# Value projection of a hybrid decoder block: four of six jobs as seven block products, a layer norm by token halves, and multiplications of the merge on GpSimd

## The chip, the cores and the metric

The kernel runs on one core of a Trainium2 chip. Its engines work at the same time, each through its own list of instructions in order: TensorE (PE in the profile, with its weight loads as PEld), VectorE (DVE), ScalarE (ACT), GpSimd (POOL) and SyncE (SP), which issues nearly all transfers between the on-chip memory (SBUF) and device memory. TensorE writes its products into eight banks of a second memory (PSUM), which VectorE and ScalarE read. The metric is the device time of one execution in microseconds. Of three runs of the kernel before the median is 1675.62 us (1674.95 to 1675.65). What VectorE can compute and what the scheduling helpers do is told below as far as the change touches it.

## The reference

One decoder layer on 1024 tokens of width 1024. What matters here is its first half:

```python
h = rms_norm(x, g_pre_mix[l])
z = h @ w_in[l]
q, k, v, glu_in, z_ga, z_gc = jnp.split(z, ...)     # v: 1024 x 1536
y_attn = dilated_attention_mixer(q, k, v, ...)       # 3 groups x 8 heads of 64, windows of 128 keys
y_conv = conformer_conv_mixer(glu_in, ...)           # GLU, causal depthwise conv, layer_norm, silu, @ w_conv_out
merged = sigmoid(z_ga) * y_attn + sigmoid(z_gc) * y_conv
x = x + rms_norm(merged @ w_mix_out[l], g_post_mix[l])
x = x + rms_norm(swiglu_ffn(rms_norm(x, g_pre_ffn[l]), ...), g_post_ffn[l])
```

The three attention groups have their own outputs per head; they are merged per head and token with weights that come from the softmax denominators. The layer norm of the convolution branch takes mean and variance over the 1024 channels of each token.

## The kernel before, in words

**Precision.** All matrix products are float32 products made of three: each operand is split in a high part (a copy rounded to the type fp32r, made by ScalarE) and a low part (operand minus high part, made by VectorE or GpSimd). A product is high by high, high by low and low by high. So each operand costs one copy and one subtraction before TensorE may use it.

**Seven products for eight.** The projections for the convolution input, the gates, the queries and the keys, and the first feed-forward matrix, use Winograd's form of Strassen's scheme (`winograd`, `prod`): a matrix product is cut in 2 x 2 blocks, and seven block products of sums of blocks replace eight. The sums of the token operand (named T1 to T4, with B11, B21, B22) are made once, in `block_sums`, and kept in `B.T`; the sums of the weights (S1 to S4, with A11, A12, A22) are made for each pair of weight tiles in `quarters`, with the splits in `both`.

**Order.** The program writes the instructions of all engines in the order of TensorE's work. TensorE's loops call `tick()` after every few products. A list of steps due at a tick (`later`), and generators that go one step further at ticks (`bg`), put the other engines' work and the transfers between them. The attention is a generator of its own, `fine`: `beat()` is called several times for each product of the value, gate and convolution-output stages, adds RATE to a credit, and for each whole credit the attention goes one step further. RATE is RV in the value stage and RU after it. Each engine then runs its list in order, whatever the others do, and waits by semaphore where its data are not there.

**The part of the program around the change**, in TensorE's order:

- Query and key projections (`qk_pair`), with the last of the depthwise convolution on VectorE beside them.
- The value stage: six jobs (`v`), each the values of one group and four of its heads, 1024 tokens by 1024 features by 256 columns. For each of eight blocks of 128 tokens it does eight steps of the features (L1139, L1140): the token block's high part is the stationary operand against 512 moving columns (the weights' high and low part side by side, made by `value_weights`), and its low part against the 256 high columns. ScalarE copies the bank (L1150), GpSimd adds the two halves (L1161), and SyncE stores the values in the layout that the group's attention reads.
- `conv_norm`, a generator in the value stage: the layer norm of the convolution's eight channel blocks, each loaded whole (128 channels by 1024 tokens). Mean, squares, their sums, `rstd` (a few small products, a square root with a Newton step, transposes that spread the result), the multiplication, and silu; the results go to device memory (`d_act`).
- The attention (`attention` with `att_s`, `att_e`, `att_t`, `att_p`, `att_o`), which starts when the layer norm is done: 96 pipelined steps. A step has the scores (L1262, L1266), their minimum on VectorE (L1270), the exponential on ScalarE (L1280), transposes of the scores of four steps before (L1305), the split of the transposed ones (ScalarE L1312, VectorE L1313), the products with the values (L1339), and the addition of the two parts of the result (ScalarE L1354, VectorE L1370). GpSimd prepares the keys (`double`, L1078 to L1080) and the values (`value_parts`, L1110, L1111). Its steps are strewn among the products of the value stage, of one more gate (`plain_gate`) and of the first part of the convolution output.
- The convolution output (`unit`, L336 to L338, 16 units of 24 products), with the silu results loaded and split by `conv_split` and the weights split by `part` (L196, L197).
- `merge`, four generators, one for each pair of heads: the three groups' outputs are loaded again, each multiplied by its weights (L1442, L1446, L1456) and added (L1451, L1461), and the sum is split (`both`, L214, L215) into `OT`. They may multiply only once the attention has ended, in turn.
- The attention output (`unit` again, 16 units of 12 products), which needs all four `OT` from its first unit on: the fourth step of the features reads `OT[3]`. Then the mixing product (L2026), norms, and the feed-forward part.

The lines that hold the value stage's products and its feed:

```python
nc.tensor.matmul(ps, a, w, start=kt == 0, stop=kt == KT - 1, skip_group_check=True)           # L1139
nc.tensor.matmul(ps[:, 256:], b, w[:, :256], start=False, stop=kt == KT - 1, ...)             # L1140
```

## Time and profile before

| what | value |
|---|---|
| median of three runs | 1675.62 us |
| profiled execution, its own time | 1676.75 us |
| its span, first to last instruction | 1675.0 us |
| granted TensorE clock | 0.999 |
| busy share of the span | PE 99%, PEld 83%, DVE 76%, ACT 49%, POOL 32% |
| value stage begins, first L1139 | 544.2 us |
| first attention step, first L1262 | 608.5 us |
| convolution output begins | 792.2 us |
| attention output begins, first product with `OT` | 901.0 us |

The page counts a product as busy from its start to a modelled end. In the value stage one that starts every 0.12 to 0.24 us has a length of 0.28 to 0.40 us, so products overlap in the record, and 99% busy does not mean that none could start earlier. What TensorE does in a stretch is better told by the distance from start to start. A window of the profile with busy time, number of instructions, and idle time before each group shows the other engines.

### The profile page before, as it was taken

To read this page: it belongs to the slowest core of one execution; us is meant where nothing else is said; L and a number is where in the kernel's file an instruction comes from. 1 tells how busy PE (TensorE), PEld (TensorE's weight loads), DVE (VectorE), ACT (ScalarE), POOL (GpSimd) and SP (SyncE) were. 2 spreads that over 40 slices of the span, in tenths; PEclk is the share of its full clock that TensorE was granted. 3 is DMA by queue.
4 is the path that set the end of the run, shared out by engine and by line. 5 is a ranking of instruction groups with operands and counts; after the bars stand their busy time and mean duration, and the time that the engine had idled before them with its cause. 6 is when DMAs were issued, how large, how long until landed. Compare 5 with 4: busy or idle time off the path is not lost.

```text
span 1675.0 us, 23388 instructions
## 1 busy us (share of the span) xinstructions
PE 1658.9 (99%) x8027; PEld 1384.6 (83%) x8027; DVE 1272.3 (76%) x2268; ACT 828.3 (49%) x1646; POOL 542.5 (32%) x456
## 2 busy tenths in 40 slices
PE   9999999999999999999999999999999999999998
PEld 7787888888888889988788888888888888888886
DVE  7998987789899768778876746877655566576686
ACT  7454443443444588888713357633333333354453
POOL 0038777787876366877300300000000000000000
PEclk9999999999999999999999999999999999999999
DMA  4435433455566987879998524134232223494334
GB/s 182 153 102 187 143 132 126 153 176 192 177 176 161 286 273 224 257 220 286 297 272 310 176 88 171 56 132 151 84 118 94 95 95 119 165 375 120 115 119 157
DMA packets 165178, 289.64 MB, mean 173 GB/s; under 512 B 47689, under 2 KB 79812, under 8 KB 165060
## 3 DMA queue, kind: packets, MB, share of 16 engines
q1 hardware_dynamic: 164420, 287.45, 52.5%
q8 instruction: 63, 1.03, 0.3%
q14 instruction: 55, 0.45, 0.1%
q10 hardware_dynamic: 288, 0.52, 0.1%
q0 software_dynamic: 352, 0.18, 0.1%
HBM read 197.39 MB, written 95.42 MB: 175 GB/s over the span
## 4 chain that ended last, share of the span: by engine, by line
PE 87%; issue 5%; DVE 2%; POOL 2%; ACT 2%; DMA 1%; SPq 0%; DVEq 0%; ACTq 0%; POOLq 0%
PE p L354 16%; PE p L353 16%; PE p L352 16%; PE p L2282 13%; PE p L2026 5%; PE p L1139 5%; PE p L336 2%; PE p L337 2%; PE p L338 2%; PE p L1140 2%; PE p L655 2%; PE p L1339 2%; PE p L1305 1%; PE p L1266 1%; PE p L1262 1%
## 5 line engine op out<-in xcount | busy, mean ns | idle before, releaser
L352 PE MATMUL p<-b,b 128*128 128x512 f32 x1316 | 512.7, 390 | 0.1
L354 PE MATMUL p<-b,b 128*128 128x512 f32 x1316 | 512.4, 389 | 0.2
L353 PE MATMUL p<-b,b 128*128 128x512 f32 x1316 | 512.2, 389 | 0.1
L352 PEld LDWEIGHTS p<-b,b 128*128 128x128 f32 x1316 | 247.1, 188 | 52.7 <-ACT c L411 0.5
L354 PEld LDWEIGHTS p<-b,b 128*128 128x128 f32 x1316 | 247.1, 188 | 52.5 <-POOL b L215 1.5
L353 PEld LDWEIGHTS p<-b,b 128*128 128x128 f32 x1316 | 247.1, 188 | 51.7 <-DVE b L1477 0.5
L2282 PE MATMUL p<-b,b 128*128 128x512 f32 x924 | 209.6, 389 | 0.0
L2282 PEld LDWEIGHTS p<-b,b 128*128 128x128 f32 x924 | 173.5, 188 | 36.0
L868 DVE SCALAR_TENSOR_TENSOR p<-b,par,p 128x511 f32<-128x511 f32 (+14 forms) x232 | 163.6, 738 | 0.0
L1139 PE MATMUL p<-b,b 128*128 128x512 f32 x384 | 144.2, 408 | 0.1
L214 ACT CAST b<-d 128x1024 fp32r<-128x1024 f32 x82 | 86.1, 1050 | 100.7 <-POOL d L237 56.6
L215 POOL TENSOR_TENSOR b<-d,b 128x1024 fp32r<-128x1024 f32 x43 | 104.2, 2422 | 47.6 <-ACT b L214 39.0
L1477 DVE TENSOR_TENSOR b<-b,b 128x512 fp32r<-128x512 f32 x141 | 98.9, 708 | 16.0 <-ACT b L1476 14.4
L215 DVE TENSOR_TENSOR b<-d,b 128x1024 fp32r<-128x1024 f32 x39 | 47.6, 1221 | 79.3 <-ACT b L214 79.3
L1140 PE MATMUL p<-b,b 128*128 128x256 f32 x384 | 107.7, 280 | 0.0
L1476 ACT CAST b<-b 128x512 fp32r<-128x512 f32 x141 | 86.4, 619 | 40.9 <-PE p L2282 18.5
L336 PE MATMUL p<-b,b 128*128 128x512 f32 x240 | 96.3, 401 | 0.0
L214 ACT CAST b<-b 128x1024 fp32r<-128x1024 f32 x51 | 53.6, 1052 | 85.0 <-POOL b L246 38.7
L1280 ACT ACTIVATE c<-c,stat 128x128 f32<-128x128 f32 (+1 forms) x192 | 85.2, 447 | 18.2 <-DVE stat L1270 16.9
L337 PE MATMUL p<-b,b 128*128 128x512 f32 x240 | 93.6, 390 | 0.0
L338 PE MATMUL p<-b,b 128*128 128x512 f32 x240 | 93.6, 390 | 0.0
L2026 PE MATMUL p<-b,b 128*128 128x512 f32 x384 | 89.9, 392 | 0.0
(248 smaller groups left out, 2897.0 us busy)
## 6 DMA issues: line engine op xcount, KB each, us to landing
b<-w_in SPq DMA_DIRECT2D x33, 512.0 KB, 5.8
b<-w_fi SPq DMA_DIRECT2D x29, 512.0 KB, 4.4
d<-w_in SPq DMA_DIRECT2D x25, 512.0 KB, 4.2
dk<-c SPq DMA_DIRECT2D x48, 256.0 KB, 4.3
dq<-c SPq DMA_DIRECT2D x48, 256.0 KB, 3.6
b<-dk SPq DMA_DIRECT2D x48, 256.0 KB, 6.2
d<-w_fi SPq DMA_DIRECT2D x22, 512.0 KB, 3.5
dqS<-c SPq DMA_DIRECT2D x44, 256.0 KB, 2.1
```

The costliest lines, as they stand in the source:

```text
L214: self.nc.scalar.copy(hi, x)
L215: self.wsplit.tensor_tensor(lo, x, f(hi), op=OP.subtract)
L336: nc.tensor.matmul(ps, hi[:, s], a, start=kt == 0, stop=False)
L337: nc.tensor.matmul(ps, hi[:, s], b, start=False, stop=False)
L352: nc.tensor.matmul(ps, hi[:, s], a, start=first and kt == 0, stop=False, skip_group_check=True)
L353: nc.tensor.matmul(ps, hi[:, s], b, start=False, stop=False, skip_group_check=True)
L354: nc.tensor.matmul(ps, lo[:, s], a, start=False, stop=kt == 3, skip_group_check=True)
L868: nc.vector.scalar_tensor_tensor(A[i][:, j:], src[i][:, :H - j], w[i], A[i][:, j:], op0=OP.mult, op1=OP.add)
L1139: nc.tensor.matmul(ps, a, w, start=kt == 0, stop=kt == KT - 1, skip_group_check=True)
L1140: nc.tensor.matmul(ps[:, 256:], b, w[:, :256], start=False, stop=kt == KT - 1, skip_group_check=True)
L2026: nc.tensor.matmul(banks[tt][nh], st, wt[:, nh * H:(nh + 1) * H], start=bool(kt == 0 and a), stop=bool(kt == KT - 1 and b))
L2282: nc.tensor.matmul(acc[t], x, y, start=first and e == 0, stop=last and e == 2, skip_group_check=True)
```

## The change

Parts of it:

- **Four value jobs by seven block products** (`QUADS = 2`, new functions `quad_load`, `quad_sum`, `quad_split`, `quad_first`, `quad_prod`, `quad`). Two jobs are the two column halves of a block product; features and tokens are halved as well. `B.T` is kept past the query and key projections, since its sums of tokens are used again. Each block product has 4 feature steps and 4 token blocks of 128, with three products of 256 columns each: the stationary operand is a token block, the moving one is the weight quarter. The weights' sums are made on VectorE, their high parts on ScalarE and their low parts on GpSimd, the first ones within the last query-and-key pair. Results leave PSUM by ScalarE and VectorE, and no GpSimd addition is needed; they are stored in pieces of 256 tokens.
- **The layer norm by token halves**: it loads 128 channels by 512 tokens, and goes twice through its steps, now in the time of the block products. Loads and stores have half the size and double the number.
- **The last two value jobs** stay as they were. The attention starts with them, its rates go from 0.42 to 0.45 and from 0.8 to 0.88, and the layer norm is done before.
- **GpSimd takes work**: in the gate and convolution-output stages the low parts of the weights (`eased`, `wsplit`), which VectorE made; in `merge` two of three multiplications; and, by `wsplit`, the low part of `OT`.

The diff, cut to its core:

```diff
-RV, RU = 0.42, 0.8
+RV, RU = 0.45, 0.88
+QUADS = 2
...
-        (nc.vector if c == 0 else self.wsplit).tensor_tensor(lo[:, s], r[:, s], f(hi[:, s]), op=OP.subtract)
+        (nc.vector if c == 0 and not self.eased else self.wsplit).tensor_tensor(lo[:, s], r[:, s], f(hi[:, s]), op=OP.subtract)
...
+    def quad_split(self, q, name):
...
+        hi, lo = self.slot(F32R), self.slot(F32R)
+        nc.scalar.copy(hi, x)
+        nc.gpsimd.tensor_tensor(lo, x, f(hi), op=OP.subtract)
...
+    def quad_prod(self, ps, w, rhs, first):
+        nc = self.nc
+        hi, lo = w
+        for kt in range(4):
+            a, b = rhs[kt]
+            n = slice(kt * 256, (kt + 1) * 256)
+            for c in range(4):
+                o = ps[c // 2][:, c % 2 * 256:(c % 2 + 1) * 256]
+                t = slice(c * 128, (c + 1) * 128)
+                nc.tensor.matmul(o, a[:, t], hi[:, n], start=first and kt == 0 and c % 2 == 0, stop=False,
+                                 skip_group_check=True)
+                nc.tensor.matmul(o, a[:, t], lo[:, n], start=False, stop=False, skip_group_check=True)
+                nc.tensor.matmul(o, b[:, t], hi[:, n], start=False, stop=kt == 3 and c % 2 == 1, skip_group_check=True)
+                if c % 2:
+                    self.tick()
...
+        X, Z = two(), two()
+        self.quad_prod(X, w.pop("A11"), operands("B11"), True)
+        x1 = copy(X, ja)
+        self.quad_prod(Z, w.pop("A12"), operands("B21"), True)
+        add(Z, x1, ja, 0)
+        Z = x1 = None
+        self.quad_prod(X, w.pop("S2"), operands("T2"), False)
+        x2 = copy(X, ja)
+        V = two()
+        self.quad_prod(V, w.pop("S1"), operands("T1"), True)
+        v1 = copy(V, jb)
+        self.quad_prod(X, w.pop("S3"), operands("T3"), False)
+        add(X, v1, jb, 1)
+        v1 = None
+        self.quad_prod(V, w.pop("S4"), operands("B22"), False)
+        add(V, x2, ja, 1)
+        V = x2 = None
+        self.quad_prod(X, w.pop("A22"), operands("T4"), False)
...
     def merge(self, hp, st, last):
...
-        nc.vector.tensor_tensor(z, z, w, op=OP.mult)
+        nc.gpsimd.tensor_tensor(z, z, w, op=OP.mult)
...
-        nc.vector.tensor_tensor(w, w, x, op=OP.mult)
+        nc.gpsimd.tensor_tensor(w, w, x, op=OP.mult)
...
     def conv_norm(self):
...
+        for hf in range(2):
+            mean, means[hf] = means[hf], None
+            q = []
+            for b in range(10):
+                if b < 8:
+                    add(A[hf, b], A[hf, b], mean, op=OP.subtract)
...
+            pb = yield from self.rstd(q[0], H, self.eps_ln, 6)
...
-    B.T = None
...
+    for i, q in enumerate(B.quads):
+        if i == QUADS - 1:
+            B.later(27, lambda: B.load_ahead(vs[0][0]))
+            B.later(30, lambda: next(att))
...
+        B.quad(q, B.T, B.quads[i + 1] if i + 1 < QUADS else None)
+    B.T = None
...
+    B.fine = att
     for i, (g, hg) in enumerate(vj):
...
     B.RATE = RU
+    B.eased, B.wsplit = True, nc.gpsimd
...
-    for n, hf in [(n, hf) for hf in range(2) for n in range(3)] + [(n, hf) for n in range(3, 8) for hf in range(2)]:
+    for n, hf in [(n, hf) for hf in range(2) for n in range(2)] + [(n, hf) for n in range(2, 8) for hf in range(2)]:
...
+    B.eased = False
```

The order of the instructions shows two of the places. First TensorE at the start of the value stage; p is a PSUM bank, the first name behind the arrow is the moving operand and the second the stationary one. Before:

```order
L1139 MATMUL p_4880<-b_4800,b_631 128x512
L1140 MATMUL p_4880<-b_4800,b_631 128x256
L1139 MATMUL p_4880<-b_4800,b_642 128x512
L1140 MATMUL p_4880<-b_4800,b_642 128x256
L1139 MATMUL p_4880<-b_4820,b_652 128x512
L1140 MATMUL p_4880<-b_4820,b_652 128x256
```

and now, where b_4818 and b_4819 are the high and the low part of a weight quarter:

```order
L1220 MATMUL p_4874<-b_4818,b_631 128x256
L1222 MATMUL p_4874<-b_4819,b_631 128x256
L1223 MATMUL p_4874<-b_4818,b_631 128x256
L1220 MATMUL p_4874<-b_4818,b_631 128x256
L1222 MATMUL p_4874<-b_4819,b_631 128x256
L1223 MATMUL p_4874<-b_4818,b_631 128x256
L1220 MATMUL p_4875<-b_4818,b_631 128x256
L1222 MATMUL p_4875<-b_4819,b_631 128x256
```

Pairs of 512 and 256 columns have become triples of 256 columns: 672 products of 256 columns stand where 256 of 512 and 256 of 256 stood for the same four jobs.

Second, GpSimd at the end of the convolution output, up to the first weights of the attention output. Before (mrg is the small tile with the merge's weights, dw their copy in device memory):

```order
L1402 TENSOR_TENSOR stat_8115<-stat_8115,mrg_8991 128x24x2
L1408 TENSOR_TENSOR mrg_8991<-mrg_8991 128x3x8x2
L1402 TENSOR_TENSOR stat_8429<-stat_8429,mrg_9131 128x24x2
L1419 DMA dw_240<-mrg_8991 48x128
L1408 TENSOR_TENSOR mrg_9131<-mrg_9131 128x3x8x2
L1419 DMA dw_241<-mrg_9131 48x128
L197 TENSOR_TENSOR b_9596<-b_9518,b_9595 128x256
```

and the last rows of the same stretch now, where L1598 and L1608 are the multiplications of a merge, L219 the low part of an `OT`, and L201 the low part of a weight tile:

```order
L1571 DMA dw_241<-mrg_9499 48x128
L1608 TENSOR_TENSOR b_9570<-b_9570,b_9559 128x1024
L201 TENSOR_TENSOR b_9660<-b_9545,b_9659 128x512
L219 TENSOR_TENSOR b_9674<-b_9654,b_9673 128x1024
L1598 TENSOR_TENSOR b_9607<-b_9607,b_9615 128x1024
L201 TENSOR_TENSOR b_9660<-b_9545,b_9659 128x512
L1608 TENSOR_TENSOR d_9103<-d_9103,b_9664 128x1024
L201 TENSOR_TENSOR b_9745<-b_9639,b_9744 128x256 x2
L219 TENSOR_TENSOR b_9772<-b_9754,b_9771 128x1024
L1598 TENSOR_TENSOR b_9708<-b_9708,b_9716 128x1024
L1608 TENSOR_TENSOR d_9357<-d_9357,b_9762 128x1024
L219 TENSOR_TENSOR b_9814<-b_9811,b_9813 128x1024
```

GpSimd's list between the last attention step and the attention output now holds eight multiplications, four low parts of `OT`, and the low parts of the weights; the last row is the low part of `OT[3]`. The last product of the attention stands in the eleventh unit after the value stage (the two of the gate and nine of the convolution output), where it stood at the end of the sixth.

More of the change, by code (lines that the diff above doesn't have):

```diff
@@ L184, in load_ahead @@
             self.sent += 1
+    eased = False
     def part(self, i, c):
@@ L321, in pair @@
             self.queued = n + 2
+        elif n < len(J) and J[n][2] == "values":
+            self.quad_first(self.quads[0], (2, 9, 3, 4, 19, 20, 22, 25))
         elif n < len(J):
@@ new lines, in quad, with ordered, plain, operands @@
+    def quad(self, q, T, then):
+        nc, w = self.nc, q["w"]
+        last = then is None
+        def ordered(x, g):
+            if g == 0:
+                return x.rearrange("p (e t c) -> p t e c", e=2, t=2)
+            return x.rearrange("p (t e c) -> p t e c", t=2, e=2)
+        def plain(ps):
+            return ps.rearrange("p (t e c) -> p t e c", t=2, e=2)
+        def operands(name):
+            return T.pop(name) if last else T[name]
+        def store(x, job, hf):
+            (g, hg), done = job
+            for b in range(2):
+                i = 4 * hf + 2 * b
+                for e in range(2):
+                    d = self.d_v[g, 2 * hg + e]
+                    if g == 0:
+                        nc.sync.dma_start(d[:, i * 128:(i + 2) * 128], x[b][:, e * 256:(e + 1) * 256])
+                    else:
+                        nc.sync.dma_start(d.rearrange("(t p) c -> p t c", p=128)[:, i:i + 2], ordered(x[b], g)[:, :, e])
+        def result():
+            if not last or "S2" in w:
+                return [self.half(), self.half()]
+            x = self.slot()
+            return [x[:, :H], x[:, H:]]
+        def copy(ps, job):
+            x = result()
+            for b in range(2):
+                d = ordered(x[b], job[0][0])
+                if job is ja:
+                    nc.scalar.copy(d, plain(ps[b]))
+                else:
+                    nc.scalar.activation(d, plain(ps[b]), AF.Identity, scale=-1.0)
+            return x
+        def add(ps, x, job, hf):
+            for b in range(2):
+                d = ordered(x[b], job[0][0])
+                if job is ja:
+                    nc.vector.tensor_tensor(d, plain(ps[b]), d, op=OP.add)
+                else:
+                    nc.vector.tensor_tensor(d, d, plain(ps[b]), op=OP.subtract)
+            self.later(4, lambda: store(x, job, hf))
+        def two():
+            return [self.bank(), self.bank()]
+        ja, jb = q["jobs"]
+        for k, step in ((1, lambda: self.quad_split(q, "A12")), (5, lambda: self.quad_sum(q, "S4")),
+                        (9, lambda: self.quad_split(q, "S2")),
+                        (17, lambda: self.quad_split(q, "S1")), (25, lambda: self.quad_split(q, "S3")),
+                        (33, lambda: self.quad_split(q, "S4")), (41, lambda: self.quad_split(q, "A22"))):
+            self.later(k, step)
+        if then:
+            self.quad_first(then, (34, 42, 31, 32, 49, 45, 47, 55))
+        X, Z = two(), two()
[16 more added lines that the diff above has]
+        self.quad_prod(X, w.pop("A22"), operands("T4"), False)
+        o = result()
+        for b in range(2):
+            nc.scalar.activation(ordered(o[b], jb[0][0]), plain(X[b]), AF.Identity, scale=-1.0)
+        def end():
+            store(o, jb, 0)
+            self.vn = jb[1] + 1
+        self.later(3, end)
@@ L1489, in conv_norm @@
         nc = self.nc
-        mean = self.slot()
-        A = []
-        def load():
-            A.append(self.slot())
-            nc.sync.dma_start(A[-1], self.d_conv[len(A) - 1])
-        for _ in range(4):
-            load()
-        yield 3
-        for hf in range(2):
-            s = slice(hf * H, (hf + 1) * H)
-            ps = self.bank("s")
-            nc.tensor.matmul(ps, self.mean_col.to_broadcast([128, 128]), self.csum[:, s], start=True, stop=True)
-            nc.scalar.copy(mean[:, s], ps)
+        add = nc.vector.tensor_tensor
@@ new lines, in conv_norm, with load, average @@
+        A = {}
+        def load(hf, j):
+            x = self.slot()
+            for e in range(2):
+                b = 2 * j + e
+                nc.sync.dma_start(x[:, e * H:(e + 1) * H], self.d_conv[b][:, hf * H:(hf + 1) * H])
+                A[hf, b] = x[:, e * H:(e + 1) * H]
+        def average(hf):
+            ps = self.bank()
+            nc.tensor.matmul(ps, self.mean_col.to_broadcast([128, 128]), self.csum[:, hf * H:(hf + 1) * H],
+                             start=True, stop=True)
+            m = self.half()
+            nc.scalar.copy(m, ps)
+            return m
@@ L1505, in conv_norm @@
+        for j in range(4):
+            self.later((1, 3, 8, 11)[j], lambda j=j: load(0, j))
+        yield 5
+        means = [average(0), average(1)]
         self.csum = None
         yield 1
[L1507 to L1520 removed]
```

121 lines of the change are left out of this document (75 added, 46 removed).

## The prediction

> **What bounds the kernel now.** First the busy shares, then the windows of the stages that the change touches, then the distances between products on TensorE.
>
> ```profile
> PE 1658.9 (99%) x8027; PEld 1384.6 (83%) x8027; DVE 1272.3 (76%) x2268; ACT 828.3 (49%) x1646; POOL 542.5 (32%) x456
> ...
> 544.20:594.40 50.20, 49.91 (x285) 42.71 (x286) 37.46 (x35) 28.98 (x40) 16.96 (x14) 1.00 0.85 270
> 594.40:631.00 36.60, 34.99 (x231) 31.05 (x230) 23.49 (x66) 30.04 (x74) 23.73 (x29) 1.00 0.94 281
> 631.00:770.20 139.20, 137.85 (x1040) 127.05 (x1038) 110.96 (x385) 119.76 (x375) 104.48 (x147) 1.00 0.81 239
> 770.20:835.40 65.20, 62.09 (x400) 52.49 (x399) 58.69 (x184) 53.66 (x168) 30.48 (x41) 1.00 0.99 302
> 835.40:901.00 65.60, 65.60 (x293) 54.13 (x291) 46.94 (x53) 14.78 (x25) 3.44 (x6) 1.00 0.91 273
> ```
>
> A window's row gives its length, then the busy time of PE, PEld, DVE, ACT and POOL, the granted clock and the transfers' share. The first is the first two value jobs, the next three run from the third job to the attention's end, the last is the rest of the convolution output. TensorE is nearly always busy, at full clock. In the attention's main part ACT is busy for 119.76 of 139.2 us and DVE for 110.96, so they run close behind it. At the end GpSimd has 3.44 us of work in 65.6: it is free there.
>
> Busy time hides gaps, so I price products by the distance of starts.
>
> ```profile
> 599.67 0.40 PE L1139 MATMUL p<-b,b 128*128 128x512 f32 x1
> 599.91 0.28 PE L1140 MATMUL p<-b,b 128*128 128x256 f32 x1
> ...
> 603.20 0.40 PE L1139 MATMUL p<-b,b 128*128 128x512 f32 x1
> ...
> 663.26 0.40 PE L1266 MATMUL p<-b,b 128*128 128x256 f32 x2
> 663.50 0.49 PE L1305 MATMUL p<-ident,c 128*128 128x128 f32 x3
> ...
> L2282 PE MATMUL p<-b,b x924: 388/389/389, 1458.3 to 1667.5; 128*128 128x512 f32 x185
> ```
>
> Ten pairs of 512 and 256 columns lie between 599.67 and 603.20: 353 ns a pair. A product of 512 columns takes (1667.5 − 1458.3)/923 = 227 ns, so the 256 columns of a pair cost 126. The two of L1266 start 0.24 us before the next row, 118 or 120 ns each; I take 118. Three transposes last 0.49 where one lasts 0.275 (the row below): 108 ns each. Products of 128 columns I estimate at half of 118, 59 ns.
>
> **What the attention loses.** Its products, from 594.4 to 835.4:
>
> ```profile
> L1140 PE MATMUL p<-b,b 128*128 128x256 f32 x257 | 72.1, 280 | 0.0
> L1305 PE MATMUL p<-ident,c 128*128 128x128 f32 x280 | 46.9, 275 | 0.2 <-DVE c L1313 0.2
> L1339 PE MATMUL p<-c,b 128*128 128x128 f32 x152 | 30.8, 250 | 0.9 <-ACT c L1312 0.4 <-POOL b L1111 0.3
> L1339 PE MATMUL p<-c,b 128*66 128x128 f32 x152 | 25.4, 227 | 3.3 <-DVE c L1313 3.0
> L336 PE MATMUL p<-b,b 128*128 128x512 f32 x49 | 21.6, 440 | 0.0
> L1339 PE MATMUL p<-c,b 128*128 128x256 f32 x64 | 21.4, 334 | 0.0
> L1339 PE MATMUL p<-c,b 128*66 128x256 f32 x64 | 18.1, 282 | 0.0
> L1266 PE MATMUL p<-b,b 128*128 128x256 f32 x88 | 17.9, 283 | 0.2 <-POOL b L1080 0.2
> L1266 PE MATMUL p<-b,b 128*128 128x128 f32 x104 | 17.5, 250 | 0.0
> L1262 PE MATMUL p<-b,b 128*128 128x256 f32 x60 | 17.2, 294 | 1.3 <-POOL b L1079 1.3
> L1262 PE MATMUL p<-b,b 128*128 128x512 f32 x40 | 16.2, 405 | 0.2 <-DVE stat L1270 0.2
> ```
>
> Attention: 280 × 0.108 = 30.5, 408 of 128 columns × 0.059 = 24.1, 276 of 256 × 0.118 = 32.6, 40 of 512 × 0.227 = 9.1; together 96.3 us. Around it 257 pairs × 0.353 = 90.7, and six units of 24 products (145 with the first row of a seventh) × 0.227 = 32.9. Work 219.9 of 241.0 us: 21.1 lost, 8.8%; the waits that the rows name, ended by DVE, ACT and POOL, make some 6 of it, and the rest is in distances. An error in the small products' prices hardly matters, since they stand on both sides.
>
> **The block products.** They take away four jobs, 256 pairs × 0.353 = 90.4 us, and put 672 products × 0.118 = 79.3 in their place; as the triple is a row not seen in a long run, its bounds are half of 227 (76.3) and the 126 of a pair (84.7). 118 is the only one measured between products of 256 columns. The first two jobs took 50.2 for 128 × 0.353 = 45.2, so 5.0 went to the norm's small products and to waits. The norm now lies wholly beside the block products; I keep 5.0: 84.3 us. The engines have room: if they do in it, as an estimate, the 37.46, 28.98 and 16.96 us of the first window once more by half, and the weights' sums and splits (13 copies of 1.05, 13 low parts of 2.42, rows below), none comes above 60 of 84.
>
> By the Trainium skill, "TensorE: Matmul & The Clock Gate", section "Back-to-back issue gap", 256 columns take 256/2.4 + 2.5, about 109 ns, which would make the 672 products 73.3 us by estimate. The 227 of the last row above, where that formula gives 216, speak for the higher price.
>
> **The attention.** It now begins after the block products, with 128 pairs (45.2), and ends in the eleventh unit: 246 products × 0.227 = 55.8. With its own 96.3 that is 197.3. It is the same 96 steps in less TensorE work, so each engine's share rises. GpSimd loses additions (L1161) and gains low parts of weights, which come off DVE; the norm, which filled the window's first 14 us (to the first L1262 at 608.5), is gone from it. I take these as even, so the same 8.8% is lost: 197.3/0.912 = 216.3. Bounds: half the loss (206), or the loss of its late part (second rival).
>
> **The rest of the convolution output.** 18 units (two of the gate, 16) less 10.25 leave 7.75 × 24 × 0.227 = 42.2 us, where 65.6 stood.
>
> **The merges.** They may multiply only after the attention, and that stretch has become shorter while work went to the slower engine.
>
> ```profile
> L215 POOL TENSOR_TENSOR b<-d,b 128x1024 fp32r<-128x1024 f32 x43 | 104.2, 2422 | 47.6 <-ACT b L214 39.0 <-issue 6.5 <-POOL b L256 1.5
> L197 POOL TENSOR_TENSOR b<-b,b 128x512 fp32r<-128x512 f32 x8 | 12.4, 1572 | 13.2 <-ACT b L196 8.7 <-PE p L338 4.5
> L197 POOL TENSOR_TENSOR b<-b,b 128x256 fp32r<-128x256 f32 x7 | 5.3, 761 | 73.5 <-ACT b L196 73.5
> ...
> L1461 DVE TENSOR_TENSOR b<-b,b 128x1024 f32<-128x1024 f32 x2 | 4.2, 2123 | 0.0
> ...
> L214 ACT CAST b<-d 128x1024 fp32r<-128x1024 f32 x82 | 86.1, 1050 | 100.7 <-POOL d L237 56.6
> ...
> 890.04 1.23 DVE L215 TENSOR_TENSOR b<-b,b 128x1024 fp32r<-128x1024 f32 x1 [0.66 <-ACT b L214]
> ...
> 901.02 0.39 PE L336 MATMUL p<-b,b 128*128 128x512 f32 x1
> ```
>
> Before, the low part of `OT[3]` came at 891.3 and was first read after 901: ten us to spare. Now GpSimd has, up to it, eight multiplications and four low parts of 128x1024 (12 × 2.42 = 29.1), six low parts of 512 columns (9.4), two of 256 (1.5), and small ones of about 2.4: 42.4 us. Its last step waits for DVE's addition and ACT's copy (2.12 + 1.05 = 3.2), and three earlier such chains show perhaps 1.5 each: 50 us. TensorE needs it 42.2 + 3 × 3 × 0.227 = 44.3 us after the attention's end, so it waits about 6. Bounds: 1, if the list is closed up, and 11, if every chain shows in full and the multiplications wait for `dw`. Behind that wait stands all of TensorE's later work.
>
> **Sum.** 84.3 + 216.3 + 42.2 + 6 = 348.8 against 50.2 + 241.0 + 65.6 = 356.8 measured: −8.0. The profiled execution took 1676.75 (span 1675.0 and 1.75 around), 1.13 above the median; on the median this gives 1667.6, so **1668**.
>
> **Rivals.**
>
> *GpSimd is in time.* The four chains overlap with the weights' parts and nothing waits at the attention output: 1667.6 − 6 = about 1662. For it: 42.4 is under 44.3. Against: 1.9 us cannot hold even the last chain of 3.2.
>
> *The attention's helpers become the bound (slower).* The last stretch, 770.2 to 835.4, where the attention ran beside 512-column products as nearly all of it would now, loses more:
>
> ```profile
> L1305 PE MATMUL p<-ident,c 128*128 128x128 f32 x68 | 12.1, 275 | 0.0
> L1339 PE MATMUL p<-c,b 128*128 128x128 f32 x45 | 9.7, 255 | 0.4 <-ACT c L1312 0.4
> L1339 PE MATMUL p<-c,b 128*66 128x128 f32 x45 | 7.9, 234 | 2.7 <-DVE c L1313 2.4
> L1339 PE MATMUL p<-c,b 128*128 128x256 f32 x13 | 4.4, 342 | 0.0
> ...
> 534.43 1.32 DVE L1005 TENSOR_TENSOR c<-c,c 128x512 fp32r<-128x512 f32 x1
> ...
> 536.97 0.68 DVE L208 TENSOR_TENSOR b<-b,b 128x512 fp32r<-128x512 f32 x1
> ...
> 533.91 1.30 POOL L256 TENSOR_TENSOR b<-b,b 128x512 fp32r<-128x512 f32 x1
> ```
>
> 68 × 0.108 + 90 × 0.059 + 26 × 0.118 (the second form of 256 columns as often as the first) + 145 × 0.227 = 48.7, and the window's other 71 products, scores, at 0.059 to 0.118 about 6.4: 55 of 65.2, 15.6% lost, with DVE busy for 58.69. If the whole window loses that, it takes 197.3/0.844 = 233.8, 17.5 more: 1685. The mechanism is DVE and GpSimd in each other's way: the same DVE subtraction took 1.32 us beside a GpSimd operation and 0.68 alone, and more GpSimd work stands beside the attention. The change stops paying above 224.3 us. Against: taking the weights' low parts off DVE relieves the engine that was 90% busy there.
>
> The Trainium skill, "SBUF — State Buffer", section "SBUF: two separate sides", says that a VectorE operation with two SBUF inputs and a GpSimd operation share a port pair that one holds for a whole instruction. The 1.32 against 0.68 agree with it.
>
> *The block products are starved.* The norm's loads and stores are half as large and twice as many.
>
> ```profile
> b<-dconv SPq DMA_DIRECT2D x7, 512.0 KB, 6.0
> b<-w_v SPq DMA_DIRECT2D x5, 512.0 KB, 8.4
> ```
>
> A block product lasts 5.7 us, less than the 6.0 or 8.4 us of a transfer. If one late weight load (8.4) stops TensorE with the norm's transfers queued ahead of it on SyncE: 1676, no gain. Against: loads are issued a pair of jobs ahead, and the transfers' share there was 0.85, not full.
>
> *The weight loads are not hidden.* The load record of a product lasts some 190 ns. One after the other, 672 × 0.19 = 127.7 instead of 79.3 gives 1716. Against it: two loads per 353 ns already overlap in the pairs above.
>
> The Trainium skill, "TensorE: Matmul & The Clock Gate", section "The mechanism", lets a load go ahead of a running product only into rows not in use or into a background buffer; products here use all rows, and the pairs' distance shows the latter.
>
> **How the numbers follow.** The forecast has 0.55, with its own range 1663 (wait 1) to 1674 (wait 11, loss 9.2%); GpSimd in time 0.17; starved 0.14; helpers as bound 0.13; loads not hidden 0.01. The range 1659 to 1681 takes in the first three, with two to three us for the block products' bounds on the low side, and stops short of the others. A measurement of this kernel tells 0.2%, 3.35 us, from no change. Faster than 1672.3: most of the forecast (0.45) and GpSimd in time (0.17), 0.62. Within: the forecast's slow end (0.10) and most of the starved case, 0.23. Slower than 1679.0: 0.15.
>
> **What would show it.** Block products: L1220, L1222 and L1223 start 118 ns apart and the last comes 84 us after the first; gaps there released by a weight load or a low part mean the starved case. Attention: 216 us from the first remaining value job to its last product; 234, with DVE's two-input rows longer, means the second rival. Merges: PE idle some 6 us before a step with the last `OT`, released by GpSimd's L219; no such row means GpSimd was in time. Wrong would be a gain or loss outside these stretches: from the attention output on I expect every distance unchanged.

## The result, and the profile after

The changed kernel takes 1698.95 us (median of four, 1697.85 to 1700.43) against 1675.63: a ratio of 1.014, 95% interval 1.0123 to 1.0158. It is slower by 1.4%, where a gain to 1668 was forecast. The profiled execution's span is 1698.6 us.

The page of the changed kernel, busy shares and chain; then a table of windows (length, then busy time of PE, PEld, DVE, ACT, POOL, granted clock, transfers' share, GB/s): block products, attention, the units behind it, the wait, the attention output.

```profile
PE 1660.6 (98%) x8187; PEld 1393.8 (82%) x8187; DVE 1281.1 (75%) x2270; ACT 831.3 (49%) x1647; POOL 612.4 (36%) x484
...
PE 44%; DVE 1%; DMA 1%; issue 1%; POOL 0%; ACT 0%; DVEq 0%; SPq 0%; POOLq 0%; ACTq 0%
...
546.40:641.80 95.40, 87.55 (x701) 85.62 (x699) 66.70 (x83) 54.88 (x79) 45.05 (x27) 0.98 0.66 206
641.80:865.90 224.10, 216.25 (x1507) 192.84 (x1508) 181.24 (x613) 183.95 (x583) 156.60 (x212) 0.98 0.92 264
865.90:910.20 44.30, 42.93 (x192) 35.03 (x191) 30.34 (x27) 10.83 (x19) 35.10 (x22) 1.00 0.98 289
910.20:924.00 13.80, 3.31 (x12) 1.74 (x10) 8.74 (x5) 2.11 (x4) 8.99 (x5) 0.67 0.86 322
924.00:967.50 43.50, 43.50 (x183) 35.80 (x184) 32.86 (x52) 14.46 (x30) 7.96 (x9) 0.95 0.62 213
```

The same windows of the kernel before, first attention step to last, and from there to the low part of `OT[3]`:

```profile
608.50:835.40 226.90, 220.83 (x1585) 198.38 (x1583) 185.88 (x625) 191.69 (x599) 155.29 (x214) 1.00 0.88 261
835.40:891.30 55.90, 55.90 (x251) 46.09 (x249) 44.11 (x48) 11.20 (x17) 2.71 (x5) 1.00 0.93 269
```

From the start of the value stage to the start of the mixing product the kernel before takes 400.3 us (544.2 to 944.5) and the changed one 421.1 (546.4 to 967.5), where 392.3 was forecast. The rest of the 23.6 between the spans lies outside: 2.1 before the value stage and 0.7 behind the mixing's start. The 2.1 are not the change's (`all_dve`, with the same code up to there, begins the stage at 544.7), and the profiled run is itself 1.5 above its median.

What TensorE waited for in the changed kernel (us in total, times, longest), and the rows of the three largest waits:

```profile
PE p L342 <- ACT b L218: 8.6, 1, 8.6
PE p L1222 <- POOL b L1201: 3.6, 2, 2.7
PE p L1146 <- ACT b L1310: 3.4, 1, 3.4
...
606.10 0.39 PE L1222 MATMUL p<-b,b 128*128 128x256 f32 x1 [2.69 <-POOL b L1201]
...
638.20 0.28 PE L1223 MATMUL p<-b,b 128*128 128x256 f32 x1
641.84 0.80 PE L1146 MATMUL p<-b,b 128*128 128x512 f32 x1 [3.36 <-ACT b L1310]
...
921.56 0.80 PE L342 MATMUL p<-b,b 128*128 128x512 f32 x1 [8.60 <-ACT b L218]
923.98 0.80 PE L343 MATMUL p<-b,b 128*128 128x512 f32 x1 [1.62 <-POOL b L219]
```

TensorE reaches the attention output at 910.2, does three steps, and stands until `OT[3]` is there: its high part lets L342 go at 921.56, its low part, ready at 923.9, lets L343 go. The granted clock is 0.67 in that window and below full behind it. The low part came 58.0 us after the attention's last product (865.9), against 55.9 before; but where 65.6 us of products covered the 55.9, 44.3 stood against the 58.0.

The page's chain, followed back from the last instruction, is mostly TensorE's (44% of the span) down to 924.0. Ahead of that it goes through the last merge: a transfer of its weights, GpSimd's two multiplications, VectorE's addition and ScalarE's copy (within "issue"), and GpSimd's low part. Its main pieces:

```profile
901.62 9.39 DMA b<-dw
...
912.13 2.35 POOL b L1598
914.48 2.30 POOL d L1608
916.77 4.77 issue
...
921.59 2.35 POOL b L219
...
923.98 0.80 PE p L343
```

It can't be followed further back than 899. That the path runs on through the attention to the block products is read from start times: the attention's first step comes 34.8 us later than before (643.3 for 608.5) and `OT[3]` 32.6 later (923.9 for 891.3).

### The profile page after: what moved, and what is told of

Its sections match the earlier page's. It is cut to its first block, busy times and chain, and to the rows that moved or that the text cites. A ratio compares the mean times of both kernels' runs of the same rounds, so it can differ in the third digit from the quotient of the medians.

```text
span 1698.6 us, 23834 instructions
## 1 busy us (share of the span) xinstructions
PE 1660.6 (98%) x8187; PEld 1393.8 (82%) x8187; DVE 1281.1 (75%) x2270; ACT 831.3 (49%) x1647; POOL 612.4 (36%) x484
## 5 line engine op out<-in xcount | busy, mean ns | idle before, releaser
L358 PE MATMUL p<-b,b 128*128 128x512 f32 x1316 | 513.2, 390 | 0.8 <-DVE c L1032 0.7
L360 PE MATMUL p<-b,b 128*128 128x512 f32 x1316 | 512.9, 390 | 0.3
L359 PE MATMUL p<-b,b 128*128 128x512 f32 x1316 | 512.6, 390 | 0.1
L358 PEld LDWEIGHTS p<-b,b 128*128 128x128 f32 x1316 | 247.1, 188 | 53.4 <-DVE c L1032 1.5
L360 PEld LDWEIGHTS p<-b,b 128*128 128x128 f32 x1316 | 247.1, 188 | 52.9 <-POOL b L219 1.5
L359 PEld LDWEIGHTS p<-b,b 128*128 128x128 f32 x1316 | 247.1, 188 | 51.4 <-DVE b L1629 0.5
L2454 PE MATMUL p<-b,b 128*128 128x512 f32 x924 | 209.9, 389 | 0.1
L2454 PEld LDWEIGHTS p<-b,b 128*128 128x128 f32 x924 | 173.4, 188 | 36.5 <-DVE c L2341 0.6
L219 POOL TENSOR_TENSOR b<-d,b 128x1024 fp32r<-128x1024 f32 x43 | 104.1, 2421 | 47.6 <-ACT b L218 39.0
L1629 DVE TENSOR_TENSOR b<-b,b 128x512 fp32r<-128x512 f32 x141 | 102.9, 737 | 16.8 <-ACT b L1628 15.1
L342 PE MATMUL p<-b,b 128*128 128x512 f32 x240 | 99.4, 414 | 8.6 <-ACT b L218 8.6
L219 DVE TENSOR_TENSOR b<-d,b 128x1024 fp32r<-128x1024 f32 x39 | 47.6, 1221 | 79.3 <-ACT b L218 79.3
L1628 ACT CAST b<-b 128x512 fp32r<-128x512 f32 x141 | 86.5, 620 | 42.6 <-PE p L2454 18.3
L219 POOL TENSOR_TENSOR b<-b,b 128x1024 fp32r<-128x1024 f32 x28 | 67.4, 2407 | 98.5 <-ACT b L218 98.5
L218 ACT CAST b<-b 128x1024 fp32r<-128x1024 f32 x51 | 53.7, 1052 | 100.0 <-POOL b L250 40.5
L343 PE MATMUL p<-b,b 128*128 128x512 f32 x240 | 95.5, 398 | 1.9 <-POOL b L219 1.9
L344 PE MATMUL p<-b,b 128*128 128x512 f32 x240 | 95.2, 397 | 1.4 <-POOL b L201 1.4
L2198 PE MATMUL p<-b,b 128*128 128x512 f32 x384 | 90.0, 392 | 0.0
L2198 PEld LDWEIGHTS p<-b,b 128*128 128x128 f32 x384 | 71.4, 188 | 14.4
```

The lines of the kernel that those rows point to most:

```text
L218: self.nc.scalar.copy(hi, x)
L219: self.wsplit.tensor_tensor(lo, x, f(hi), op=OP.subtract)
L342: nc.tensor.matmul(ps, hi[:, s], a, start=kt == 0, stop=False)
L343: nc.tensor.matmul(ps, hi[:, s], b, start=False, stop=False)
L344: nc.tensor.matmul(ps, lo[:, s], a, start=False, stop=kt == nk - 1)
L358: nc.tensor.matmul(ps, hi[:, s], a, start=first and kt == 0, stop=False, skip_group_check=True)
```

## The experiments

Times are medians, each beside runs of the kernel before at 1675 to 1677. "OT[3] after" is the time from the attention's last product to the end of `OT[3]`'s low part; "window" runs from the first value job behind the block products to the attention's last product.

**Is it GpSimd?** `mult_dve` puts the multiplications back (below), `all_dve` also the low parts (`eased` off, `wsplit` VectorE); `before_gp` gives them to GpSimd in the kernel before.

```diff
-        nc.gpsimd.tensor_tensor(z, z, w, op=OP.mult)
+        nc.vector.tensor_tensor(z, z, w, op=OP.mult)
-        nc.gpsimd.tensor_tensor(w, w, x, op=OP.mult)
+        nc.vector.tensor_tensor(w, w, x, op=OP.mult)
```

> The two multiplications of a merge that went to GpSimd are back on VectorE; all else as in the changed kernel (1698.95). Theory A, GpSimd is what makes the last OT late: eight operations of 2.4 us leave its list and VectorE does them in 1.25, so OT[3]'s low part comes some 10 us or more earlier and the 15 us that TensorE stood at the attention output shrink to 5 or less: 1685 to 1689. Theory B, the merges take about 56 us after the attention whichever engine multiplies (in the kernel before 891.3 - 835.4 = 55.9, now 923.9 - 865.9 = 58.0), because their loads and the buffers set the pace: OT[3] comes 2 to 4 us earlier: 1694 to 1698.

> All work that went to GpSimd is back on VectorE: the two multiplications, the low parts of OT and the low parts of the weights in the gate and convolution-output stages. Block products, norm by halves and rates as in the changed kernel. Theory A: the wait at the attention output is gone, but the attention, with VectorE fuller, takes some 5 us longer: about 1690. Theory B: the wait stays at 8 us or more, since the attention still ends only 42 us of TensorE work before the attention output, and the time is 1692 to 1700. If VectorE bounds the attention, its window grows from 224 to over 230 us.

> The kernel before with two of three multiplications of each merge and the low part of OT on GpSimd, and nothing else changed: 65.6 us of TensorE work stand behind its attention, and OT[3] was 10 us early. Theory A: the merges take 10 us or more longer, the slack is used up and TensorE waits: 1677 to 1682. Theory B: OT[3] comes at most 4 us later, no wait: 1675 to 1676.

Measured: 1694.44, 1691.47 and 1676.33 (ratio of the last 1.0, 0.999 to 1.0009). OT[3] after: 56.3, 52.5 and 56.5 us. In the windows from the attention's end to `OT[3]`, in that order:

```profile
864.20:920.50 56.30, 45.56 (x201) 36.83 (x199) 42.05 (x39) 13.10 (x22) 22.61 (x18) 0.93 1.03 292
...
864.50:917.00 52.50, 45.60 (x202) 36.86 (x200) 43.24 (x51) 12.93 (x22) 2.97 (x6) 0.96 1.02 304
...
834.70:891.20 56.50, 56.50 (x254) 46.63 (x254) 45.95 (x38) 12.40 (x20) 30.07 (x16) 1.00 0.91 272
```

In the kernel before, GpSimd's share goes from 3 to 30 us of work and the merges' length by 0.6: the edit costs nothing there, where 65.6 us of products cover it. In the changed kernel the multiplications are worth 1.7 us of `OT[3]`'s time and the low parts 3.8 more (those of `OT` and of the weights are not told apart). Theory A, with its ten us and more, falls. Theory B's times held or were missed by under a us, but the wait it put at 8 us or more is 6.4 in `all_dve`. Taking GpSimd's work away gains 7.5 of the 23 us, 6.5 of them between the attention's end and the mixing product. The attention's window stays at 224.3 us:

```profile
640.20:864.50 224.30, 217.47 (x1508) 193.99 (x1509) 185.52 (x623) 184.62 (x583) 145.40 (x201) 0.98 0.93 264
```

**What paces the merges?** `one_spread` loads one third of the weights.

```diff
-        w = self.spread(hp, 1)
+        w = x
-        x = None
-        x = self.spread(hp, 2)
```

> all_dve with one of the three loads of merge weights (dw, spread over the partitions, 512 KB each) for each merge; the second and third multiplication use the first one's weights, so the merged values are not those of the model. Same VectorE, ScalarE and GpSimd work. Theory B in its sharper form, the transfers set the pace of the merges (52.5 us after the attention's end): OT[3] comes 10 us or more sooner and the wait at the attention output nearly goes: 1680 to 1683. If VectorE's own work or the order of the steps sets it: OT[3] at 49 to 53 us, 1688 to 1692.

Measured: 1690.24, OT[3] after 49.1 us.

```profile
862.30:911.40 49.10, 45.45 (x201) 36.74 (x199) 42.99 (x51) 12.94 (x22) 2.90 (x6) 0.99 0.76 265
```

The transfers' share falls from 1.02 to 0.76, and `OT[3]` comes 3.4 us sooner, not ten (1.2 us of the whole time). VectorE is busy for 42.99 of the 49.10: its own work is nearly the length of the merges, and as long as the 42.6 us of products that cover them here. Transfers add a little, and the sharper form of theory B falls. That VectorE's work sets the rest fits the range but has no run of its own.

**More cover by a faster attention?** `ru100` has RU = 1.0 for 0.88, `cover` is `all_dve` with 1.12, `before_rates` the kernel before with 0.45 and 0.88.

> The changed kernel with the attention's second rate at 1.0 for 0.88, so that the attention ends about one unit sooner in the order and more of the convolution output is left behind it. Theory B (what is short is TensorE work behind the attention to cover the merges): about 6 us more cover, the wait at the attention output falls by as much: about 1692. Theory C (the attention's window is bound by its helper engines): the window's length hardly falls though a unit of work has left it, the gain in the wait is given back there: 1697 to 1701. Theory A expects the same as B or less.

> The kernel of all_dve (all GpSimd work of the change back on VectorE, 1691.5) with the attention's second rate at 1.12 for 0.88. With 1.0 for 0.88 the attention ended 27 products sooner in the order and its window lost 5.8 us, no more than those products cost. Theory B: 45 to 50 products, some 10 us, move behind the attention; OT[3] still comes about 52 us after the attention's end, and the wait of some 10 us at the attention output is down to nothing: 1680 to 1683. Theory C, the helper engines bound the attention: the window falls by less than half of the 10 us: 1686 to 1692.

> The kernel before with the rates of the changed one (0.45 and 0.88 for 0.42 and 0.8) and nothing else. Theory F: the attention starts at 608 as before, its chain of 272 to 283 us ends at 880 to 891 with slack, TensorE bounds: 1675 to 1677, and OT[3] comes up to 10 us sooner. If denser attention costs TensorE time by itself, as in the run with 1.12: 1678 to 1682.

Measured: 1694.33, 1690.03, 1678.64 (ratio of the last 1.0017, 1.0005 to 1.0029). In `ru100` the window falls by 5.8 us, about the price of the 27 products that left it, and the wait of 8.6 to 4.9: theory B's way, though the time lies between the two ranges. In `cover` 54.2 us of products stand behind the attention and `OT[3]` comes after 52.8: the wait is gone. But the window falls only from 224.3 to 220.7 us although some 51 products (11.6 us) left it; theory C holds there. Rates alone gain the kernel before nothing, as its `OT[3]` was early. Of the 0.2% they cost, the profiled run has 0.3 us ahead of the mixing product and some 2 behind it, so a loss within the attention is not shown.

**The start of the attention.** `before_late` is `before_rates` with the attention begun at `i == 1` for `i == 0` in the value stage.

> The kernel before with its attention begun after the second value job instead of the first, and with the changed kernel's rates (0.45 and 0.88); no block product in it. Theory F: from the first attention step to the low part of OT[3] the helper engines need 272 to 284 us in every kernel so far (before 608.5 to 891.3, changed 643.3 to 923.9, all_dve 641.7 to 916.9), and the changed kernel is slower because its attention starts 35 us later. Here it starts 15 to 24 us later, OT[3] is ready at 900 to 915, where TensorE wants it at about 903: a wait at the attention output, and 1677 to 1688. If instead the block products themselves are the loss, nothing is lost here: 1675 to 1677.

Measured: 1691.74. It doesn't test what it should: the attention started only 10 us later, all of it TensorE's wait of 11.1 us for the late loads of the keys:

```profile
PE p L1262 <- DMA b<-dk: 11.1, 1, 11.1
```

`OT[3]` was ready at 896.5, before TensorE wanted it at 913.7. The loss is that wait and what follows it. The run is inconclusive on theory F.

**The block products.** `quad_fix` is `all_dve` with three edits:

```diff
-            if not last or "S2" in w:
+            if not last or self.first1:
...
-            nc.scalar.activation(ordered(o[b], jb[0][0]), plain(X[b]), AF.Identity, scale=-1.0)
+            if b:
+                nc.scalar.activation(ordered(o[b], jb[0][0]), plain(X[b]), AF.Identity, scale=-1.0)
+            else:
+                nc.vector.tensor_scalar(ordered(o[b], jb[0][0]), plain(X[b]), -1.0, None, op0=OP.mult)
...
-            if hf:
-                nc.scalar.activation(rs[:, :1], self.eps_ln, AF.Exp)
```

(`first1` is true for a pair's first result alone.)

> all_dve with three edits in the block products that leave their arithmetic as it is: the first result of the last pair of jobs is held in two half buffers for one whole one, so that a whole buffer is left for the low part of S2; the last two results leave PSUM by VectorE and ScalarE for ScalarE alone; and the early exponential that loads ScalarE's table is gone. If the 95.5 us of the block products are long for want of a buffer (2.85 us and the lower clock after it) and for ScalarE's list at the end (3.5 us and the lower clock after it), they take 86 to 90 us, and the time is 1683 to 1687. If other waits take their place (VectorE's list at the end, transfers): 93 us or more, 1689 to 1692.

Measured: 1684.13. The stage takes 89.0 us for 95.5, at full clock, and the wait of 2.69 is gone (one of 0.9 for a low part stays):

```profile
546.30:635.30 89.00, 85.83 (x702) 84.09 (x700) 64.61 (x83) 52.44 (x76) 43.36 (x24) 1.00 0.70 217
...
635.29 0.50 PE L1146 MATMUL p<-b,b 128*128 128x512 f32 x1 [1.35 <-ACT b L1313]
```

The attention starts 7.2 us sooner after the stage's start than in `all_dve` (89.8 for 97.0), and the time is 7.3 us less. This fits theory F, by which the chain from the attention's first step to `OT[3]` sets the time; but it is no test of it, as TensorE's own stage is shorter by as much. Nor is the size sure: the unedited stage took 94.0 us in `cover`, `split_early` and `one_spread`, so the edits are worth 5.0 to 6.5 us. In the changed kernel GpSimd stands idle for 8.6 us, until VectorE's L1274 is done, before it makes the low part that L1222 waits for; that the wait goes with a buffer more speaks for the buffer, though the three edits were made together. ScalarE's list shows the wait of 3.36: the last results (L1310) stand behind the norm and a table load:

```profile
603.70 2.35 POOL L1201 TENSOR_TENSOR b<-b,b 128x1024 fp32r<-128x1024 f32 x1 [8.60 <-DVE b L1274]
...
637.97 0.81 ACT L1690 ACTIVATE b<-b,par 128x512 f32<-128x512 f32 x1
638.80 1.28 ACT L1699 ACT_TABLE_LOAD   x1
640.09 0.20 ACT L1699 ACTIVATE c<-eps_ln 128x1 f32<-128x1 f32 x1
640.20 0.60 ACT L211 CAST b<-b 128x512 fp32r<-128x512 f32 x1
640.71 1.07 ACT L1310 ACTIVATE b<-p 128x512 f32<-128x512 f32 x2
```

**Work moved within the attention.** `split_early` starts `conv_split` in the first of the two value jobs.

> all_dve with the loading and splitting of the convolution's silu results (16 halves on ScalarE and VectorE) begun in the first of the two remaining value jobs, for the second. Theory D: the attention's window is long (12% lost, 13 of 27.5 us between 739 and 800) because this work stands in the stretch of the gate and the first units: the window falls from 224 to 216 to 219 us, and as OT[3] follows the attention's end, the whole time falls as much: 1683 to 1687. If ScalarE and VectorE are simply full over the whole window, the loss moves into the value stage: 1690 to 1692.

Measured: 1702.80, window 231.1 us. Both ranges are missed and theory D falls: the work costs more where it was moved to. What it costs there wasn't followed; one wait of TensorE, 3.4 us for keys from GpSimd, is part of it.

**What sets the attention's length?** `combo1` is the changed kernel with the edits of `quad_fix`, multiplications and `OT` on VectorE, the weights' low parts left on GpSimd, and rates 0.52 and 1.0; `combo2` has 0.6 and 1.0.

> The changed kernel with the three edits of quad_fix, the merges' multiplications and the low parts of OT on VectorE, the weights' low parts left on GpSimd, and rates 0.52 and 1.0. Against quad_fix (1684.1) VectorE has some 5 us less beside the merges, and the attention ends sooner in the order. Theory F: what counts is the chain from the first attention step to OT[3], 272 us in quad_fix: it falls to 260 to 266, and TensorE's wait of 6 us goes: 1675 to 1680. If GpSimd beside VectorE slows it as much as it relieves it: 1682 to 1686.

> combo1 with a first rate of 0.6 for 0.52: more of the attention beside the two value jobs, where TensorE lost only 6.9% (21% in the first stretch after them). If the helper engines have room there, the chain shortens by some 5 us more and TensorE takes over as the bound: 1673 to 1677. If they have none, the loss in the value jobs rises by what the later stretch gains: within 2 us of combo1.

Measured: 1681.38 and 1688.22. The first lies between its two ranges: the chain is 268.8 us and TensorE's wait at the attention output is gone, but the kernel stays 0.3% behind. So the chain to `OT[3]` is not all of the loss. The second misses both. The windows:

```profile
633.80:849.70 215.90, 205.75 (x1453) 182.20 (x1454) 178.23 (x614) 182.09 (x581) 153.69 (x212) 1.00 0.94 269
...
634.10:849.20 215.10, 200.94 (x1420) 176.73 (x1421) 176.72 (x612) 181.81 (x581) 152.86 (x211) 1.00 0.92 265
```

At the higher rate 33 products, some 7.5 us, leave the window, and its length falls by 0.8; they stand behind it instead, and the whole time is 6.8 us longer. VectorE and ScalarE are busy for 177 to 184 us in these two and in the changed kernel's window alike. In `combo1` they also wait for each other:

```profile
DVE c L1470 <- ACT c L1469: 32.7, 44, 1.1
...
ACT c L1437 <- DVE stat L1427: 18.9, 28, 1.3
```

178 us of work and 33 of waiting for ScalarE make VectorE's 211 of 216. Two runs take work out of `combo1`, `act_light` by the first hunk and `dve_light` by the other two:

```diff
-                                 bias=st[:, hh:hh + 1], accum_out=st[:, 2 + hh:3 + hh])
+                                 bias=st[:, hh:hh + 1], **({} if hh else dict(accum_out=st[:, 2:3])))
+        nc.gpsimd.memset(st[:, 3:4], 1.0)
...
+            nc.gpsimd.memset(self.O, 0.0)
...
-        for h in range(2):
+        for h in range(1):
```

> combo1 with less work for ScalarE in the attention: the exponentials of the second head of each pair are not summed (a constant stands for the sum, so the output is not the model's), which takes away 96 accumulator reads of 0.19 us, 18 us of the 181 that ScalarE is busy in the attention's 215 us. GpSimd writes the constant, 96 small operations more. If ScalarE sets the attention's length (184 us busy of 224 in the changed kernel, 181 of 215 in combo1 and combo2, whatever the rate): 198 to 206 us from the first value job to the attention's last product. If VectorE or the latency of a step sets it: 212 to 216. The whole time follows only as far as the merges let it.

> combo1 with less work for VectorE in the attention: of the two additions that put the parts of a result together (0.55 us each in the profile, 94 rows in all) only that of the first head is made, and zeros stand for the second head, so the output is not the model's. That takes some 26 of the 177 us that VectorE is busy. If VectorE sets the attention's length: 190 to 203 us. If ScalarE sets it: 210 to 216. If both in turn (each waits for the other within a step): 203 to 210 here and in act_light.

Measured: windows of 212.6 and 212.8 us (1677.71 and 1678.11). ScalarE's busy time fell by 8, not 18, and VectorE's by 28; they bought 3.3 and 3.1 us. So neither sets the length alone; the 203 to 210 expected if both did in turn were not reached either. The next three lengthen the distance between a step's parts, in `combo3` (below): `deep1` LT, LP = 5, 6 for 4, 5; `deep4` 4, 6; `deep5` 5, 6 with 13 half buffers for 11 and 41 whole ones for 42.

> combo3 (1679.7) with the transposes of a step five steps after its scores and the products with the values six steps after (LT, LP = 5, 6 for 4, 5), all buffers as they were. Taking 8 us of busy time from ScalarE or 28 from VectorE shortened the attention by only 3.3 us each, so neither sets its length alone. Theory L: it is the time of a step's way through the engines, on which TensorE, in its fixed order, waits; one step more between gives each part 2 us more, and the attention's window falls from 220.6 to 205 to 215 us: 1670 to 1677. If the engines are full in turn, or the half buffers run out: 218 to 224, 1678 to 1684.

> combo3 with only the products with the values a step later (LT, LP = 4, 6). The waits of TensorE that the records name in the attention are mostly of these products, for the two halves of the transposed scores (ScalarE's copy and VectorE's subtraction). Theory L, as far as it lies in that part: window 210 to 216, 1673 to 1677. If not: 218 to 224, 1678 to 1684.

> deep1 with two half buffers more (13 for 11) and one whole buffer fewer (41 for 42), so that the deeper order doesn't wait for buffers. If deep1 gains little for want of half buffers, this one gains: window 205 to 215. The block products may lose a microsecond or two by the missing whole buffer. If it is no better than deep1, buffers are not it.

Measured: 1693.45, 1689.15, 1756.38; windows 233.2, 227.8 and 231.2 us for 220.6. All three lie above both of their ranges, and theory L, as priced, falls too; want of buffers isn't excluded by `deep5`, which has fewer whole ones. In `deep5` the missing whole buffer costs some 45 us before the value stage (it starts at 589.6 for 544.9) and the block products take 106.2. What sets the window's length, 213 to 224 us in most of these kernels, stays open. VectorE and ScalarE, waiting for each other, fits the rows; no run has isolated it. Transfers, whose share is 0.94 in `combo1`'s window, had no run of their own there; they end 1.1 us of TensorE's named waits.

**A better version.** `combo3` is `combo1` with rates 0.48 and 0.94 and the third load of weights early:

```diff
         w = self.spread(hp, 1)
-        yield 7
+        yield 3
+        x2 = self.spread(hp, 2)
+        yield 4
```

> combo1 with rates between (0.48 and 0.94) and the third load of a merge's weights issued four steps after the second, ahead of the first multiplication, for which a whole buffer more is held. Rate 1.0 and 0.52 had OT[3] ready 1.5 us before TensorE wanted it, so lower rates should lose less TensorE time in the attention (14.7% there, 11.2% at the old rates) if the merges are 3 us shorter, as in one_spread: 1676 to 1679. If the loads wait for buffers or for SyncE's list anyway: 1681 to 1684.

Measured: 1679.71, ratio 1.0027 (1.0016 to 1.0038); OT[3] after 51.5 us for 53.7. It just misses its range. It has block products of 89.0 us and a window of 220.6, and is 19 us faster than the change, still 0.3% behind the kernel before; from `combo1` (1.0032, 1.002 to 1.0044) it can't be told apart.

## Why the prediction was wrong

Its sum failed in three terms; the 28.8 us between 392.3 and 421.1 are 11.1, 7.8 and 9.9 of them.

- **The merges, "50 us" and "it waits about 6".** The working added up GpSimd's list. The kernel before had OT[3] 55.9 us after the attention with GpSimd nearly idle, by the very rows that the prediction quotes (835.4 and 890.04 + 1.23); they were read as "ten us to spare", as if the ten stayed while the cover fell from 65.6 to 44.3. By them the wait is 11.6, before any edit of the merges. The list's "50 us" measured 58.0. L343, the first product that reads the low part, starts 11.5 us later than ten products of 0.227 behind 910.2 would have it (923.98 for 912.48), just over the bounds of 1 to 11; 8.6 and 1.6 of it stand in the rows as idle. The lower clock behind the wait, which the sum has at nothing, takes 2.2 more, and the rest of the convolution output 2.1 more than its 42.2, of which 1.4 is a wait for a weight's low part that stands behind a multiplication in GpSimd's list. Together it is 101.6 us from the attention's end to the mixing product where 91.7 was forecast. With GpSimd's work back on VectorE (`all_dve`) it is 95.0: that work makes 6.5 of the 9.9 us here, and nothing where the cover is longer (`before_gp`).
- **The block products, "I keep 5.0: 84.3 us".** The products came as priced: the last starts 91.8 us after the first, and in undisturbed stretches three take 0.36 us, 672 × 0.12 = 80.6. The 5.0 for all else measured near 15: waits of 2.7 and 3.4 us, each with a lower clock after it, and small ones; 8.4 are left in `quad_fix`, not followed further. The starved rival was right in part (a weight's low part late), but not by a transfer: `quad_fix` shows a buffer and ScalarE's list. The engines' shares said nothing of either; the "60 of 84" also has no price for VectorE's sums of the weights, and it was busy for 66.7.
- **The attention, "the same 8.8% is lost: 216.3".** It took 224.1, within its bounds. TensorE's work in it was as priced, with 246 products of units as forecast, so the loss was 26.8 us for 19.0 (280 × 0.108 is 30.2, not 30.5, which hardly matters). A lost share was carried over as if TensorE's work set the length. From first step to last the attention took 226.9 us before and 222.6 after (643.3 to 865.9), and 214 at the highest rates, where products of TensorE taken from beside it are worth little; the first 27 were still worth their price (`ru100`). What set the 224.1 stays open.

The range missed because these three errors add on one path, while the forecast treated the attention's start as free; the 5.0 of the block products, which had no bounds, was off the most. The second rival had the side right, slower, with the helper engines as bound; its place and price (17.5 us in the window, where 7.8 were lost) did not hold. Its mechanism, VectorE against GpSimd, isn't borne out: `all_dve`, with 11 us less of GpSimd's work and 4 more of VectorE's beside the attention, left the window as it was. As both change there, it isn't excluded. The conflict itself is real (below). "GpSimd is in time" fell with the wait; the weight loads were hidden, as forecast. Outside the stages named, distances stayed as they were, as forecast.

## What to carry to other kernels

Where one engine looks full, follow the last result backwards through all engines before work is taken off it: here the chain from the attention's start to `OT[3]` took 283 us before with ten to spare, the changed kernel starts it 35 us later, and 23 are lost. That the late start is the cause is argued from these sums: no run moved the start alone. Slack of a side chain is a difference of two numbers; when a change shortens the cover, it must be taken again from the measured chain, not from a list of one engine's work. And a busy share far below full doesn't show that a stage has room, if its list's order or its buffers decide.

## What the runs showed that was not expected

VectorE beside GpSimd was slowed far more than the 1.32 against 0.68 seen before: one addition of a merge took 5.85 us in the changed kernel, and 2.11 in `all_dve` (last row), where GpSimd does nothing meanwhile.

```profile
879.53 5.85 DVE L1613 TENSOR_TENSOR b<-b,b 128x1024 f32<-128x1024 f32 x1
...
879.72 2.38 POOL L1598 TENSOR_TENSOR b<-b,b 128x1024 f32<-128x1024 f32 x1
882.07 1.28 POOL L201 TENSOR_TENSOR b<-b,b 128x512 fp32r<-128x512 f32 x1
...
886.68 2.11 DVE L1613 TENSOR_TENSOR b<-b,b 128x1024 f32<-128x1024 f32 x1
```

The two GpSimd operations beside it last 2.38 and 1.28 us; with the 2.11 they make 5.77, as if VectorE had stood still for both. This goes with the Trainium skill, "SBUF — State Buffer", section "SBUF: two separate sides", by which one of the two engines holds the shared ports for a whole instruction.

After its wait of 8.6 us TensorE ran on at a lower granted clock: products of 512 columns started every 0.43 us until 928.4, for 0.227 at full clock. The waits of 2.7 and 3.4 us show it too, and one of 1.4 us at 902.4 doesn't. In five us each (the granted clock is the third number from the end):

```profile
605.00:610.00 5.00, 3.90 (x23) 3.90 (x24) 5.00 (x4) 0.63 (x1) 3.77 (x2) 0.76 0.52 172
640.00:645.00 5.00, 3.16 (x11) 2.87 (x12) 1.45 (x6) 2.38 (x8) 4.72 (x6) 0.67 0.87 256
900.00:905.00 5.00, 3.63 (x17) 2.67 (x16) 3.59 (x3) 0.00 (x0) 5.00 (x3) 1.00 1.02 286
925.00:930.00 5.00, 5.00 (x16) 3.96 (x15) 1.81 (x3) 0.62 (x1) 0.00 (x0) 0.65 0.75 292
```

Over the block products the clock is 0.98, and 1.00 without these waits in `quad_fix`. A wait of TensorE thus cost more than its length here, by 2.2 us behind the longest.
